# Queries and keys of the third pair of heads by seven products, with the token sums on GpSimd

## The chip, the cores and the metric

The kernel runs on one core of a Trainium2 chip. The metric is the device time of one execution in microseconds (us). In the profile the engines are PE (TensorE, the matmuls; PEld is its loading of weights), DVE (VectorE), ACT (ScalarE), POOL (GpSimd) and SP (SyncE, which issues most transfers).

## The reference

One layer of a hybrid backbone for two groups of tokens with the same weights: a prompt of 128 tokens and a sample of 512, D = 1024 channels, 16 heads of 64, all in float32. Cut to what matters:

```python
h = x * (1 + scale) + shift                        # modulation from the conditioning vector
z = h @ w_in                                       # 10 x 1024 columns: conv inputs, gates, q, k, v, merge gates
hy, g_h, qkv, g_a, m = split(z)
v_h, x1, x0 = split(short_conv(hy))                # 3 taps
y_h = (irfft(rfft(v_h * x1) * rfft(filter)) + (v_h * x1) * d_bias) * x0
q, k, v = split(qkv)
y_a = softmax(q k^T / 8 + bias, windows and context) v    # sample; the prompt attends to itself
p_h = (y_h * silu(g_h)) @ w_bh
p_a = (y_a * silu(g_a)) @ w_ba
m_h, m_a = split(sigmoid(m))
out = (m_h * p_h + m_a * p_a) @ w_out
y = layer_norm(ALPHA * x + gate * out)
```

The prompt's keys and values are outputs too.

## The kernel before

The 640 tokens are two halves of 320 columns (`HALF`, `CS`). The activations lie with channels on partitions, in 8 chunks of 128. A float32 operand is split into a high and a low part in the matmul's format (`hH`/`hL` for the tokens, `wh`/`wl` for weights), and each product is three passes: high x high, high x low, low x high. `split` makes the two parts, the high by a copy on ACT (L101), the low by a subtraction on DVE (L102).

There are two forms of projection onto a tile of 128 output channels. `proj` takes one weight tile: 8 chunks x 3 passes x 2 halves = 48 matmuls of 320 columns. `pair_tile` takes two weight tiles and both halves as a 2 x 2 block product and does it by seven products in place of eight: 7 x 4 chunks x 3 passes = 84 matmuls. It needs sums of the tokens, t1 to t4, made once and kept (`token_sums(r)`, where r = 0 or 1 picks chunks 0, 1 or 2, 3 of each half of the channels), sums of the weights (`wsum`, L1024, on DVE) with their splits, and sums of the results (L1058 to L1066, on DVE). The products come in the order `b11, t2, t3, t1, b21, t4, b22`; the split weights go round in a ring of buffers (`wh` has two, `wl` three), the raw weights have two buffers, which SP loads (`load_to`, L63).

The stages: a prologue makes h; four quarters of the convolution branch (`quarter_head`, `quarter_tail`, `long_conv`, `long_conv_back`; the products `yb` belong to the last step of the long convolution, and `conv_tile` reads a projection's result out of PSUM on ACT, L479 to L483, as zs); the hand-over; eight rounds of attention; the merge (projections `T_BH` and `T_BA`, gated by the merge gates, then the output projection); layer norm. Through the rounds `attend(j)`, two heads at a time, is woven into `mains(j)`, other projections that keep PE busy: scores (L819), probabilities (smallest value on DVE, L834; exponential on ACT, L839; reciprocal on DVE, L840; the multiply by it on GpSimd, L841, and L894 for the prompt), transposes (L859), values (L866). GpSimd does little else in this part.

The hand-over and round 0 are written so before:

```python
yield from chain(queries(0), keys(0), values(0), gate_a(0), queries(1))
yield from alongside(chain(keys(1), values(1)), token_sums(0), 2)          # end of hand_over
0: ((alongside(chain(gate_a(1), queries(2), keys(2)), token_sums(1), 2),), 3 * NK),   # mains(0)
1: ((mix(0), queries_keys(3)), 2 * N_PAIR),                                 # first pairs: round 1
```

`alongside(x, y, 2)` takes one step of y for two steps of x; `weave` spreads one chain over another by the numbers of steps given. The hand-over is woven with the end of the last long convolution.

What sets the order: each engine works through its own queue in order, and waits there for what the next instruction needs. In the rounds PE's queue is in the order written (`manual_schedule` for PE); the queues of the other engines there, and all of them in the convolution stages and the merge, are ordered by a scheduler when the kernel is built, except where `keep_in_program_order` pins an instruction. Weight tiles are named by number: `T_Q` = 32, `T_K` = 40, `T_V` = 48, `T_GA` = 56, `T_MH` = 64, `T_MA` = 72, `T_BH` = 80. The queries and keys of pair 2 are tiles 34 and 42, the first pair of the merge gates 64 and 65, gate_a(1) is tile 57.

Of the kernel before, what the change touches and what calls it, by code (L numbers as in the profile page):

```python
# [9 lines left out]
F32 = mybir.dt.float32  # L10
F32R = mybir.dt.float32r
AF = mybir.ActivationFunctionType
ALU = mybir.AluOpType
# [5 lines left out]
NK = 8  # L19
NT = 640  # L20
HALF = 320
# [24 lines left out]
def tile_hyena_natten_step(ctx: ExitStack, tc: tile.TileContext, a, o):  # L46
    nc = tc.nc
    P = 128

    def f(ap):  # L50
        return ap.bitcast(F32)
# [4 lines left out]
    def two(t):  # L56
        return t.rearrange("p (a b) -> p a b", a=2)
# [442 lines left out]
    def quarter_head(q):  # L500
        us = []
        out[f"u{q}"] = us
        for i in range(2):
            n = 2 * q + i
            u = hw.tile([P, NG + 1], F32, tag="u", bufs=4, name=f"u{n}")
            x1 = hwa.tile([P, NG + 1], F32, tag="cv", bufs=2, name=f"x1_{n}")
            yield from conv_tile(n, u)
            yield
            yield from conv_tile(8 + n, x1)
            nc.vector.tensor_tensor(u[:, :NG], u[:, :NG], x1[:, :NG], op=ALU.mult)  # L510
            us.append(u)
            yield
# [143 lines left out]
    def chain(*gens):  # L656
        for g in gens:
            yield from g
# [123 lines left out]
    def hand_over():  # L782
        yield from quarter_tail(3)
        hwa_stack.close()
        out["slots_l"] = left.enter_context(tc.tile_pool(name="slots_l", bufs=1))
        out["slots_q"] = left.enter_context(tc.tile_pool(name="slots_q", bufs=1))
        yield from chain(queries(0), keys(0), values(0), gate_a(0), queries(1))
        out["slots_r"] = left.enter_context(tc.tile_pool(name="slots_r", bufs=1))
        yield from alongside(chain(keys(1), values(1)), token_sums(0), 2)

    tail = ctx.enter_context(ExitStack())
    ac = ctx.enter_context(ExitStack())
# [172 lines left out]
    tok = {t: [[], []] for t in SUMS}  # L965

    def token_sums(r):
        def part(t, i, j):
            return f(t[:, 4 * i + 2 * r : 4 * i + 2 * r + 2, CS[j]])

        def step(dst, i, j, sign):
            for t in (hH, hL):
                nc.vector.tensor_tensor(dst, dst, part(t, i, j), op=ALU.add if sign > 0 else ALU.subtract)

        t1, t2 = (two(row(sp, "s", f"ts{r}{i}", bufs=2)[:]) for i in range(2))

        def keep(name, t):
# [4 lines left out]
            split(two(tok[name][0][r][:]), two(tok[name][1][r][:]), t)  # L982

        tc.keep_in_program_order(nc.vector.tensor_tensor(t1, part(hH, 0, 1), part(hL, 0, 1), op=ALU.add))
        yield
        nc.vector.tensor_tensor(t2, t1, part(hH, 0, 0), op=ALU.subtract)
        nc.vector.tensor_tensor(t2, t2, part(hL, 0, 0), op=ALU.subtract)
        yield
        keep("t1", t2)
        yield  # L990
        nc.vector.tensor_tensor(t1, part(hH, 1, 1), t1, op=ALU.subtract)
        nc.vector.tensor_tensor(t1, t1, part(hL, 1, 1), op=ALU.add)
        yield
        keep("t3", t1)
        yield
        step(t2, 1, 1, -1)
        yield
        keep("t2", t2)
        yield
        step(t2, 1, 0, 1)  # L1000
        yield
        keep("t4", t2)

# [6 lines left out]
    ORDER = ("b11", "t2", "t3", "t1", "b21", "t4", "b22")  # L1010
    RING = ("wh", "wl", "wl", "wh", "wl")

    def pair_tile(i0, i1, use):
        for i in (i0, i1):
            if i not in raws:
                wraw(i)
        ra, rb = raws.pop(i0), raws.pop(i1)
        a11, a12, a21, a22 = (r[:, 512 * h : 512 * h + 512] for r in (ra, rb) for h in range(2))
        src = {0: a11, 4: a12, 5: a22}
        wb = {}  # L1020

        def wsum(j, x, y, op, dst=None):
            src[j] = dst if dst is not None else row(sp, "s", f"s{j}_{i0}", bufs=2)[:, :512]
            nc.vector.tensor_tensor(src[j], x, y, op=op)  # L1024
# [7 lines left out]
        def halfrow(tag, bufs, name):  # L1032
            return sp.tile([P, 384], F32, tag=tag, bufs=bufs, name=f"{name}{i0}")[:, :HALF]

        wsum(2, a11, a21, ALU.subtract)
        wsum(1, src[2], a22, ALU.subtract)
        for j in range(3):
            prep(j)
        wsum(3, a21, a22, ALU.add)
        wsum(6, a12, src[1], ALU.add, src[1])  # L1040
        for j in range(3, 5):
            prep(j)
        ps = {}
        for j in range(7):
            if j < 4:
                ps["xyvz"[j]] = acc(f"sp{i0}_{j}")[:, :HALF]
            dst, x = ps["xyvzxvz"[j]], operand(ORDER[j])
            for k in range(4):
                wh, wl = (wb[j][:, i, P * k : P * k + P] for i in range(2))
                for i, (wk, xi) in enumerate(((wh, 0), (wh, 1), (wl, 0))):  # L1050
                    nc.tensor.matmul(  # L1051
                        dst, wk, x(xi, k), start=j < 4 and k == 0 and i == 0, stop=k == 3 and i == 2, skip_group_check=True,
                    )
                if k == 1:
                    yield
            if j == 0:
                u = halfrow("u", 1, "u")
                nc.scalar.activation(u, dst, AF.Copy)  # L1058
            elif j == 1:
                nc.vector.tensor_tensor(u, dst, u, op=ALU.add)  # L1060
            elif j == 4:
                use(0, 0, dst)
            else:
                if j != 3:
                    c = halfrow("c", 4, f"c{j}_")
                nc.vector.tensor_tensor(c, dst, c if j == 3 else u, op=ALU.add)  # L1066
                if j != 2:
                    use(*{3: (1, 1), 5: (1, 0), 6: (0, 1)}[j], c)
            prep(j + 5)
            yield  # L1070

    def queries_keys(j):
# [23 lines left out]
        yield from pair_tile(t0 + n0, t0 + n0 + 1, use)  # L1096

    N_PAIR = 14

    def alongside(main, side, every):  # L1100
# [76 lines left out]
    def gate_rows():  # L1177
        for k in range(NK):
            raw = slot(k % 2, "v", f"gate{k}")[:, :D]
            load_to(raw, a["wgate"][k])  # L1180
            yield
            for c in range(2):
                s_ = st[:, k, c : c + 1]
                if k == 0:
                    ins = nc.vector.tensor_scalar_mul(gbc[:, c], raw, s_)
                else:
                    ins = nc.vector.scalar_tensor_tensor(gbc[:, c], raw, s_, gbc[:, c], op0=ALU.mult, op1=ALU.add)
                if c == 0:
                    tc.keep_in_program_order(ins)

    wo = {}

# [24 lines left out]

    side = gate_rows()
    mhs = []
    for n in range(NK):  # L1220
        ps = now(proj(T_BH + n, yhH, yhL, dst=[[wo_row(t, 0, T_BH + n)] for t in ("woh", "wol")] if n == 2 else None))
        wraw(T_BH + n + 2)
        th = mixed(mh_d, n, "mh", NK)
        mhs.append(th)
        for p, cs in zip(ps, CS):
            gate(th[:, cs], p)
        raw = slot(1, ("q", "ql")[n % 2], f"yaraw{n}")
        load_to(raw[:], ya_d[n])
        split(yaH[n], yaL[n], raw[:])
        next(side, None)  # L1230
# [239 lines left out]
```

## Time and profile before

| | |
|---|---|
| median of 3 runs | 890.71 us (890.48 to 892.2) |
| profiled execution, its own time | 891.88 us |
| its span | 889.8 us |
| mean granted clock of TensorE in it | 0.995 |
| matmuls in the profile | 6536 with the transposes' and the attention's |
| bytes moved by DMA | 129.07 MB |

The busy share of each engine in 40 slices of the span, in tenths, shows the course: the convolution stages up to about slice 17, then the hand-over and the rounds, the merge from about slice 32.

```
PE   8999999999999999999999999999999999999996
DVE  4676693795678569698787667775777668676666
ACT  4395554645545433365666456555665632243200
POOL 0010110010101000025422322222222200000000
```

The page names an engine, a line of the kernel, an operation and "out<-in" tiles; `x12` is a count. In a list by time the first number is the start in us, the second the length of the row; in a list by groups, the numbers after the bar are the busy time in us and the mean length of one in ns. In brackets stands the idle time before and what ended it.

### The profile page before, as it was taken

How to read it: one execution, taken by the hardware profiler on the slowest of the kernel's cores; microseconds unless marked ns; L12 is line 12 of the kernel's file. 1: busy time of each engine (PE TensorE's matmuls, PEld its weight loads, DVE VectorE, ACT ScalarE, POOL GpSimd, SP SyncE). 2: the span in 40 equal slices, each digit the busy share in tenths (PEclk: the TensorE clock that was granted, in tenths of full speed). 3: DMA queues.
4: the chain of work that ended last, by engine and by line, in shares of the span. 5: the costliest groups of instructions: out<-in, count | busy, mean ns of one | idle time of the engine just before them, and what ended most of it. 6: DMA issues, size and time to landing. Idle time of an engine off the chain costs nothing.

```text
span 889.8 us, 16809 instructions
## 1 busy us (share of the span) xinstructions
PE 875.6 (98%) x6536; PEld 846.4 (95%) x6536; DVE 634.5 (71%) x1257; ACT 428.6 (48%) x912; POOL 121.6 (14%) x128
## 2 busy tenths in 40 slices
PE   8999999999999999999999999999999999999996
PEld 7899999999999999999999999999999999999885
DVE  4676693795678569698787667775777668676666
ACT  4395554645545433365666456555665632243200
POOL 0010110010101000025422322222222200000000
PEclk9999999999999999999999999999999999999998
DMA  8965665565656222263524243433252488445511
GB/s 329 395 163 122 142 141 119 143 135 120 160 113 142 72 85 76 72 193 101 157 83 141 88 139 104 148 104 113 84 169 92 140 298 283 154 153 201 209 61 58
DMA packets 53690, 129.07 MB, mean 145 GB/s; under 512 B 8267, under 2 KB 23115, under 8 KB 53612
## 3 DMA queue, kind: packets, MB, share of 16 engines
q1 hardware_dynamic: 43964, 107.72, 37.0%
q0 software_dynamic: 4032, 14.68, 10.1%
q10 hardware_dynamic: 5616, 5.61, 1.9%
q8 instruction: 51, 0.84, 0.4%
q14 instruction: 27, 0.22, 0.1%
HBM read 113.83 MB, written 14.16 MB: 144 GB/s over the span
## 4 chain that ended last, share of the span: by engine, by line
PE 91%; DMA 4%; DVE 3%; ACT 1%; issue 1%; SPq 0%; POOLq 0%; ACTq 0%; POOL 0%; DVEq 0%
PE mm L168 36%; PE sp L1051 20%; PE out L1285 6%; PE v L762 5%; PE mm L182 5%; PE pt L859 2%; DMA raw<-wall 2%; PE s L866 2%; PE s L819 2%; PE ve L774 1%; PE adaT L249 1%; DMA yhraw<-yh_d 1%; PE fl L397 1%; PE yb L158 1%; PE yb L156 1%; PE yb L157 1%
## 5 line engine op out<-in xcount | busy, mean ns | idle before, releaser
L1051 PE MATMUL sp<-t,wb 128*128 128x320 f32 x768 | 120.7, 310 | 0.1
L168 PE MATMUL mm<-hH,wh 128*128 128x320 f32 x480 | 115.0, 313 | 1.8 <-ACT zs L482 1.0
L1051 PEld LDWEIGHTS sp<-t,wb 128*128 128x128 f32 x768 | 113.8, 188 | 0.8 <-issue 0.8
L168 PE MATMUL mm<-hL,wh 128*128 128x320 f32 x480 | 114.4, 312 | 0.0
L168 PE MATMUL mm<-hH,wl 128*128 128x320 f32 x480 | 114.2, 312 | 0.0
L1051 PE MATMUL sp<-hH,wb 128*128 128x320 f32 x384 | 93.3, 313 | 1.1 <-DVE c L1066 1.1
L168 PEld LDWEIGHTS mm<-hH,wh 128*128 128x128 f32 x480 | 81.1, 189 | 3.9 <-ACT zs L482 1.2
L168 PEld LDWEIGHTS mm<-hL,wh 128*128 128x128 f32 x480 | 81.6, 189 | 1.1 <-DVE hL L326 0.5
L168 PEld LDWEIGHTS mm<-hH,wl 128*128 128x128 f32 x480 | 81.6, 189 | 0.8 <-DVE wl L102 0.4
L101 ACT ACTIVATE wh<-raw 128x1024 fp32r<-128x1024 f32 x33 | 34.8, 1058 | 73.6 <-PE mm L168 44.8
L1051 PEld LDWEIGHTS sp<-hH,wb 128*128 128x128 f32 x384 | 66.1, 188 | 3.2 <-issue 3.2
L148 POOL DMA_DIRECT2D wl<-wall x28 | 24.3, 869 | 262.7 <-ACT wl L147 225.0
L1051 PE MATMUL sp<-hL,wb 128*128 128x320 f32 x192 | 59.3, 309 | 0.0
L841 POOL TENSOR_SCALAR p<-p,sm 128x384 f32<-128x384 f32 x32 | 43.8, 1377 | 113.4 <-DVE sm L840 100.9
L102 DVE TENSOR_TENSOR wb<-s,wb 128x512 fp32r<-128x512 f32 x64 | 44.4, 699 | 20.6 <-ACT wb L101 20.5
L101 ACT ACTIVATE wb<-s 128x512 fp32r<-128x512 f32 x64 | 39.8, 628 | 34.6 <-DVE s L1024 30.6
L149 ACT ACTIVATE wh<-raw 128x1024 fp32r<-128x1024 f32 x28 | 29.7, 1061 | 52.8 <-PE mm L168 52.7
L102 DVE TENSOR_TENSOR wl<-raw,wh 128x1024 fp32r<-128x1024 f32 x33 | 40.2, 1220 | 13.6 <-ACT wh L101 13.2
L1285 PE MATMUL out<-woh,yhs 128*128 128x512 f32 (+1 forms) x176 | 45.5, 372 | 0.0
L841 POOL TENSOR_SCALAR edge<-edge,sm 128x320 f32<-128x320 f32 x32 | 41.7, 1315 | 2.6 <-DVE sm L840 2.6
L168 PE MATMUL mm<-yhs,wh 128*128 128x320 f32 x224 | 41.9, 309 | 0.0
L101 ACT ACTIVATE wb<-raw 128x512 fp32r<-128x512 f32 x48 | 30.0, 625 | 22.1 <-PE sp L1051 10.0
(357 smaller groups left out, 2155.0 us busy)
## 6 DMA issues: line engine op xcount, KB each, us to landing
raw<-wall SPq DMA_DIRECT2D x96, 512.0 KB, 3.7
wl<-wall POOLq DMA_DIRECT2D x28, 512.0 KB, 5.7
ada<-wada SPq DMA_DIRECT2D x16, 512.0 KB, 7.5
tm<-bias SPq DMA_DIRECT2D x16, 512.0 KB, 4.7
gate<-wgate SPq DMA_DIRECT2D x8, 512.0 KB, 4.4
wo<-wall SPq DMA_DIRECT2D x8, 512.0 KB, 4.3
xt<-xT SPq DMA_DIRECT2D x8, 320.0 KB, 7.5
dec<-decay SPq DMA_DIRECT2D x20, 128.0 KB, 3.3
```

What stands on the lines that cost most here:

```text
L101: hi = nc.scalar.activation(dst_h, src, AF.Copy)
L102: return hi, (eng or nc.vector).tensor_tensor(dst_l, src, f(dst_h), op=ALU.subtract)
L148: nc.gpsimd.dma_start(wl, a["wall"][i], accum_op=ALU.add)
L149: nc.scalar.activation(wh, raw[:], AF.Copy)
L168: nc.tensor.matmul(ps[hf][:, :HALF], wt[k], x[:, hf * HALF : (hf + 1) * HALF], start=(i == 0 and k == 0), stop=(i == lead[2] and k == NK - ...
L182: nc.tensor.matmul(p[:, :HALF], w[i // 2][k], (hH, hL)[i % 2][:, k, cs], start=n == 0, stop=n == len(steps) - 1, skip_group_check=True,)
L762: nc.tensor.matmul(ps[t // 2][:, t % 2 * 256 : t % 2 * 256 + 256], x[:, k, P * t : P * t + P], wk, start=first and t % 2 == 0, stop=last, ...
L819: nc.tensor.matmul(dst[h], x[rows(h), qs], y[rows(h), ks], start=i == 0, stop=i == 2, skip_group_check=True)
L841: nc.gpsimd.tensor_scalar_mul(pv, pv, sm[:, 2:3])
L859: nc.tensor.transpose(pt[:, i * P : i * P + P], x, ident)
L1051: nc.tensor.matmul(dst, wk, x(xi, k), start=j < 4 and k == 0 and i == 0, stop=k == 3 and i == 2, skip_group_check=True,)
L1285: ins = nc.tensor.matmul(dst, m[k][:, c0 : c0 + P], w[:, c : c + n], start=(first and k == 0), stop=(last and k == 5), skip_group_check=True,)
```

## The change

There are six edits.

1. Round 0 does `gate_a(1)` and then `queries_keys(2)`: the queries and keys of pair 2 as a pair by seven products, as those of pairs 3 to 7 are already.
2. The token sums of row pair 1 have to be there earlier. They are made in the hand-over, side by side with those of row pair 0 (`both`), on GpSimd in place of DVE: 18 operations of 128 x 320 (two per step of a row pair, since the temporaries are now rows of 384). The splits are in halves too: 8 copies on ACT, 8 subtractions on DVE. In the hand-over values(1) now stands ahead of keys(1).
3. `prepare` is the first part of `pair_tile`: loads of the two weight tiles, four weight sums and five splits. With the table `follow` the preparation for the following pair is issued after product 3 of the pair before, and its first weight sum is pinned in DVE's order. This holds inside the three runs of pairs that follow one another.
4. In `quarter_head` for q = 3 and i = 0 the two convolution tiles change places.
5. In the merge the first two T_BH projections are issued in a written order on PE: chunks 0 to 3 of both, then the rest.
6. `gate_rows` pins both of its operations in DVE's order, not the first alone.

```diff
@@ quarter_head
-            yield from conv_tile(n, u)
-            yield
-            yield from conv_tile(8 + n, x1)
+            tiles = ((n, u), (8 + n, x1))
+            if q == 3 and i == 0:
+                tiles = tiles[::-1]
+            yield from conv_tile(*tiles[0])
+            yield
+            yield from conv_tile(*tiles[1])
@@ hand_over
-        yield from alongside(chain(keys(1), values(1)), token_sums(0), 2)
+        yield from alongside(chain(values(1), keys(1)), both(token_sums(0), token_sums(1)), 2)
@@ token_sums(r)
+        eng = nc.gpsimd if r else nc.vector
+        if r:
+            temps = [
+                [sp.tile([P, 384], F32, tag="c", bufs=4, name=f"ts1{i}{k}")[:, :HALF] for k in range(2)] for i in range(2)
+            ]
+        else:
+            temps = [[two(row(sp, "s", f"ts0{i}", bufs=2)[:])] for i in range(2)]
...
+        def form(dst, x, terms):
+            for v, d in enumerate(dst):
+                y = x[v]
+                for t, i, j, sign in terms:
+                    eng.tensor_tensor(d, y, part(t, i, j, v), op=ALU.add if sign > 0 else ALU.subtract)
+                    y = d
...
+            for v, x in enumerate(src):
+                if r:
+                    cs = slice(HALF * v, HALF * v + HALF)
+                    split(th[:, cs], tl[:, cs], x)
+                else:
+                    split(two(th[:]), two(tl[:]), x)
...
+        form(t1, [part(hH, 0, 1, v) for v in range(len(t1))], ((hL, 0, 1, 1),))
+        form(t2, t1, ((hH, 0, 0, -1), (hL, 0, 0, -1)))
         keep("t1", t2)
+        for v, d in enumerate(t1):
+            eng.tensor_tensor(d, part(hH, 1, 1, v), d, op=ALU.subtract)
+        form(t1, t1, ((hL, 1, 1, 1),))
         keep("t3", t1)
+        form(t2, t2, ((hH, 1, 1, -1), (hL, 1, 1, -1)))
         keep("t2", t2)
+        form(t2, t2, ((hH, 1, 0, 1), (hL, 1, 0, 1)))
         keep("t4", t2)
@@ pair_tile
-    def pair_tile(i0, i1, use):
+    ready = {}
+
+    def prepare(i0, i1, pin):
         for i in (i0, i1):
             if i not in raws:
                 wraw(i)
...
-            nc.vector.tensor_tensor(src[j], x, y, op=op)
+            ins = nc.vector.tensor_tensor(src[j], x, y, op=op)
+            if pin and j == 2:
+                tc.keep_in_program_order(ins)
...
+        ready[i0] = wb, prep
+
+    def pair_tile(i0, i1, use):
...
+        if i0 not in ready:
+            prepare(i0, i1, False)
+        wb, prep = ready.pop(i0)
...
             prep(j + 5)
+            if j == 3 and (i0, i1) in follow:
+                prepare(*follow[i0, i1], True)
             yield
...
+    runs = (
+        (mix_(0), qk_(3), mix_(1), qk_(4), ga_(2)), (mix_(2), qk_(5), mix_(3), ga_(4), qk_(6)),
+        (mix_(4), qk_(7), mix_(5), ga_(6), mix_(6), mix_(7)),
+    )
+    follow = {x: y for run in runs for x, y in zip(run, run[1:])}
+
+    def both(x, y):
+        for _ in x:
+            next(y, None)
+            yield
+        yield from y
@@ mains(j)
-            0: ((alongside(chain(gate_a(1), queries(2), keys(2)), token_sums(1), 2),), 3 * NK),
+            0: ((gate_a(1), queries_keys(2)), NK + N_PAIR),
@@ gate_rows
-                if c == 0:
-                    tc.keep_in_program_order(ins)
+                tc.keep_in_program_order(ins)
@@ merge
+    firsts = [proj(T_BH + n, yhH, yhL) for n in range(2)]
+    with tc.manual_schedule(engines={mybir.EngineType.PE}):
+        for gen in firsts:
+            for _ in range(4):
+                next(gen)
+        firsts = [now(gen) for gen in firsts]
     for n in range(NK):
-        ps = now(proj(T_BH + n, yhH, yhL, dst=[[wo_row(t, 0, T_BH + n)] for t in ("woh", "wol")] if n == 2 else None))
+        if n < 2:
+            ps = firsts[n]
+        else:
+            ps = now(proj(T_BH + n, yhH, yhL, dst=[[wo_row(t, 0, T_BH + n)] for t in ("woh", "wol")] if n == 2 else None))
```

More of the change, by code (lines that the diff above doesn't have):

```diff
@@ L967, in token_sums, with part, keep @@
     def token_sums(r):
[L968 to L977, printed above, removed]
+        eng = nc.gpsimd if r else nc.vector
[5 more added lines that the diff above has]
+            temps = [[two(row(sp, "s", f"ts0{i}", bufs=2)[:])] for i in range(2)]
+        t1, t2 = temps
+        def part(t, i, j, v):
+            n = 4 * i + 2 * r
+            return f(t[:, n + v, CS[j]] if r else t[:, n : n + 2, CS[j]])
+        def form(dst, x, terms):
[4 more added lines that the diff above has]
+                    y = d
+        def keep(name, src):
             pools = [(yhp, "yh", NK + 1)] * 8 if r == 0 else [(tp, "tr", 4)] * 4 + [(sp, "tr", 3)] * 3 + [(at, "tr", 1)]
@@ L981, in keep @@
                 tok[name][i].append(row(pool, tag, f"{name}_{r}{i}", F32R, bufs))
-            split(two(tok[name][0][r][:]), two(tok[name][1][r][:]), t)
-        tc.keep_in_program_order(nc.vector.tensor_tensor(t1, part(hH, 0, 1), part(hL, 0, 1), op=ALU.add))
+            th, tl = (tok[name][i][r] for i in range(2))
+            for v, x in enumerate(src):
[5 more added lines that the diff above has]
+        form(t1, [part(hH, 0, 1, v) for v in range(len(t1))], ((hL, 0, 1, 1),))
         yield
-        nc.vector.tensor_tensor(t2, t1, part(hH, 0, 0), op=ALU.subtract)
-        nc.vector.tensor_tensor(t2, t2, part(hL, 0, 0), op=ALU.subtract)
+        form(t2, t1, ((hH, 0, 0, -1), (hL, 0, 0, -1)))
         yield
@@ L990, in token_sums @@
         yield
-        nc.vector.tensor_tensor(t1, part(hH, 1, 1), t1, op=ALU.subtract)
-        nc.vector.tensor_tensor(t1, t1, part(hL, 1, 1), op=ALU.add)
+        for v, d in enumerate(t1):
+            eng.tensor_tensor(d, part(hH, 1, 1, v), d, op=ALU.subtract)
+        form(t1, t1, ((hL, 1, 1, 1),))
         yield
@@ L995, in token_sums @@
         yield
-        step(t2, 1, 1, -1)
+        form(t2, t2, ((hH, 1, 1, -1), (hL, 1, 1, -1)))
         yield
@@ L999, in token_sums @@
         yield
-        step(t2, 1, 0, 1)
+        form(t2, t2, ((hH, 1, 0, 1), (hL, 1, 0, 1)))
         yield
@@ L1030, in prep @@
             split(wb[j][:, 0], wb[j][:, 1], src[j])
-        def halfrow(tag, bufs, name):
-            return sp.tile([P, 384], F32, tag=tag, bufs=bufs, name=f"{name}{i0}")[:, :HALF]
         wsum(2, a11, a21, ALU.subtract)
@@ L1042, in pair_tile, with halfrow @@
             prep(j)
+        ready[i0] = wb, prep
+    def pair_tile(i0, i1, use):
+        def halfrow(tag, bufs, name):
+            return sp.tile([P, 384], F32, tag=tag, bufs=bufs, name=f"{name}{i0}")[:, :HALF]
+        if i0 not in ready:
+            prepare(i0, i1, False)
+        wb, prep = ready.pop(i0)
         ps = {}
@@ L1098, in tile_hyena_natten_step, with qk_, ga_, mix_ @@
     N_PAIR = 14
+    def qk_(j):
+        return T_Q + j, T_K + j
+    def ga_(j):
+        return T_GA + j, T_GA + j + 1
+    def mix_(m):
+        t = (T_MH if m < 4 else T_MA) + 2 * (m % 4)
+        return t, t + 1
+    runs = (
[8 more added lines that the diff above has]
+        yield from y
     def alongside(main, side, every):
```

## The prediction

> **What bounds the kernel now.** I read the share of busy time first, then the chain that ended last, then the list of what TensorE (PE) waited for.
>
> ```profile
> PE 875.6 (98%) x6536; PEld 846.4 (95%) x6536; DVE 634.5 (71%) x1257; ACT 428.6 (48%) x912; POOL 121.6 (14%) x128
> PE 91%; DMA 4%; DVE 3%; ACT 1%; issue 1%; SPq 0%; POOLq 0%; ACTq 0%; POOL 0%; DVEq 0%
> ```
>
> ```profile
> engine line waited for: us in total, times, longest us
> PE adaT L266 <- POOL spare L281: 1.5, 1, 1.5
> PE sp L1051 <- DVE c L1066: 1.1, 1, 1.1
> PE mm L168 <- ACT zs L482: 1.0, 1, 1.0
> PE pt L859 <- DVE sm L834: 0.6, 1, 0.6
> ```
>
> PE is busy for 98% of the span and carries 91% of the chain. So only two things can move the time: fewer matmuls, or PE waiting less or more. Three waits behind the prologue are worth having: 1.1 us at a pair's product, 1.0 at a convolution tile and 0.6 at the attention's transposes.
>
> Shares over the whole span hide the stage that the change touches, so I looked at it by windows (columns: length, then busy time of PE, PEld, DVE, ACT, POOL).
>
> ```profile
> 372.00:397.00 25.00, 25.00 (x204) 24.37 (x204) 24.19 (x49) 11.78 (x30) 1.59 (x6) 1.00 0.58 189
> 397.00:404.80 7.80, 7.25 (x55) 6.83 (x55) 7.80 (x23) 4.20 (x11) 7.57 (x4) 1.00 0.28 77
> 404.80:415.00 10.20, 10.20 (x71) 10.10 (x72) 7.73 (x16) 5.72 (x16) 5.77 (x5) 1.00 0.31 105
> ```
>
> This is the end of the hand-over and round 0, up to the first product of pair 64. DVE works 24.19 of 25.00 us and then 7.80 of 7.80, and GpSimd (POOL) 7.57 of 7.80. PE is still full, but with two engines behind it that have nothing left. All the new work of the change falls here.
>
> **Twelve matmuls fewer.** Queries and keys of pair 2 cost 2 x 48 matmuls of 320 columns now, and 7 products x 4 blocks x 3 passes = 84 in the new form.
>
> ```profile
> 491.70 1.92 PE L1051 MATMUL sp<-t,wb 128*128 128x320 f32 x12
> 493.45 0.31 PE L1051 MATMUL sp<-hH,wb 128*128 128x320 f32 x1
> ```
>
> Twelve run from 491.70 to 493.45, 1.75 us, or 0.146 each. Gain: 12 x 0.146 = 1.75 us. That is 0.2% of the time, which is also about what a measurement of this kernel can tell from no change (1.78 us).
>
> **Stalls that the small edits take away.** The swapped order of the convolution tiles at q 3, i 0 puts other matmuls between ACT's reading of the held PSUM tile and PE's next use of it. I take all of the 1.0 us of zs L482; the cover is some fifty matmuls, and if it were gone, the 1.0 would stay.
>
> ```profile
> 574.44 0.69 DVE L1024 TENSOR_TENSOR s<-raw,raw 128x512 f32<-128x512 f32 x1 [3.86 <-DMA raw<-wall]
> 576.41 0.38 PE L1051 MATMUL sp<-hH,wb 128*128 128x320 f32 x1 [1.08 <-DVE c L1066]
> ```
>
> At 574.44 DVE stands 3.86 us before a weight sum whose tile has not landed, the combination L1066 that PE needs is queued behind it, and PE loses 1.08 us. With `prepare` the following pair's loads, sums and splits are issued after product 3 of the pair before, in a written place. The load then is earlier by about three products (some 5 us at 1.75 each), more than the 3.86, so I take the 1.1 us whole. SP's queue gets the same loads, sooner. The other pairs keep their slack: what they get earlier is one split and two sums on a DVE that isn't full there. The written order of the first two T_BH projections and the second pin in `gate_rows` touch a wait too small for the list: nothing counted, with some 0.4 us as the upper bound (an estimate, half a small wait of the list) and zero as the lower. The 0.6 us at L859 lies inside the stage that is built anew: its present form goes, and what comes in its place is the next term. Gains so far: 1.75 + 1.0 + 1.1 + 0.6 = 4.45 us.
>
> **What the hand-over has to do instead.** `token_sums(1)` leaves round 0 on DVE and becomes 18 GpSimd operations of 128x320 in the hand-over, 8 ACT copies and 8 DVE splits of half a row pair. Into DVE's queue also come the sums and splits of the weights of pair 34/42, which PE now wants at once.
>
> ```profile
> 372.12 0.28 PE L158 MATMUL yb<-ph,dftL 128*128 128x256 f32 x1
> 388.90 0.46 PE L182 MATMUL mm<-hH,wh 128*128 128x320 f32 x2
> 399.01 0.46 PE L182 MATMUL mm<-hH,wh 128*128 128x320 f32 x2
> 372.79 0.82 DVE L984 TENSOR_TENSOR ts<-hH,hL 128x640 f32<-128x640 f32 x1
> 375.24 0.82 DVE L991 TENSOR_TENSOR ts<-hH,ts 128x640 f32<-128x640 f32 x1
> 375.98 0.60 DVE L630 SCALAR_TENSOR_TENSOR u<-u,hyd,yp 128x128 f32<-128x128 f32 x2
> 394.88 0.55 DVE L834 CUSTOM_DVE_ANT_0 p<-s,tm 128x384 f32<-128x384 f32 x1
> L102 DVE TENSOR_TENSOR wb<-s,wb 128x512 fp32r<-128x512 f32 x64 | 44.4, 699 | 20.6 <-ACT wb L101 20.5
> ```
>
> The token sums follow the last `yb` of the long convolution. In the changed order of issue 113 matmuls stand between it and gate_a(1), some 14.5 us, so with gate_a(1) at 388.90 it falls at 374.4, where before it fell at 372.12: values(1), ahead of keys(1) now, fill the place. DVE starts its sums 2.3 us later. PE's frame is kept: gate_a(1) with its scores ends at 399.01, the first product of queries and keys takes 12 x 0.146, and the second wants its weights and the sums t2 at 400.8. Before that DVE has 64 operations to do, which by their rows (0.82 for a sum or split of 640, about half of that for 320, 0.70 for a weight operation of 512, 0.55 for a probability step) come to 31 us, or about 27 when overlaps of 0.07 us between neighbours are taken off (the operation of 375.24 has its successor at 375.98). 374.4 + 27 = 401.4 to 402.4: DVE alone is 0.6 to 1.6 us late, without any disturbance. I take 1.5.
>
> GpSimd's part has no such operation in the trace. The nearest are these:
>
> ```profile
> L841 POOL TENSOR_SCALAR edge<-edge,sm 128x320 f32<-128x320 f32 x32 | 41.7, 1315 | 2.6 <-DVE sm L840 2.6
> 442.19 2.14 POOL L841 TENSOR_SCALAR edge<-edge,sm 128x320 f32<-128x320 f32 x2 [0.64 <-DVE sm L840]
> 397.23 4.52 POOL L841 TENSOR_SCALAR edge<-edge,sm 128x320 f32<-128x320 f32 x2 [1.35 <-DVE sm L840]
> 401.73 6.10 POOL L841 TENSOR_SCALAR p<-p,sm 128x384 f32<-128x384 f32 x4
> 407.81 2.76 POOL L841 TENSOR_SCALAR edge<-edge,sm 128x320 f32<-128x320 f32 x2
> L1314 POOL TENSOR_TENSOR r<-r,bc 128x64 f32<-128x64 f32 x1 | 0.3, 319 | 175.9 <-ACT r L1313 175.9
> L1315 POOL TENSOR_TENSOR r<-r,bc 128x64 f32<-128x64 f32 x1 | 0.6, 612 | 0.1
> 403.42 0.82 PE L859 MATMUL pt<-pack,edge 128*128 128x128 f32 x6
> 404.79 0.93 PE L859 MATMUL pt<-pack,p 128*128 128x128 f32 x6 [0.56 <-DVE sm L834]
> 404.98 1.01 DVE L1024 TENSOR_TENSOR s<-raw,raw 128x512 f32<-128x512 f32 x1
> ```
>
> A multiply of this size takes 1.07 us alone (442.19), 1.3 on average, and (4.52 + 2.76) / 4 = 1.82 beside a full DVE; DVE's own 512-column sum is longer there too, 1.01 against about 0.70. The only two tensor-tensor rows, of 64 columns, scatter by a factor of two. So an operation costs between 1.07 and 1.82, and I take 1.5, nearer to the crowded rows since DVE is as full here. 18 x 1.5 = 27 us from 374.8: GpSimd is through at 402, where undisturbed (18 x 1.07 = 19.3) it would be at 394 or, with its two waits for DVE's splits of t1 and t2, at 396. Behind these eighteen are queued the attention's multiplies, which began at 397.23 before and feed the transposes at 403.42 and 404.79; DVE's and ACT's halves of `t*_1` wait for GpSimd in their own order, and behind ACT's halves stand the copies that free PSUM for keys(1). So GpSimd is some 5 us late for the multiplies, and what DVE loses to it, some 0.15 us for each of 18 operations (2.6 us, worked out from 0.3 us for every DVE operation that meets one, about half of them), comes partly on top. Of 1.5 + 5 + 2.6 I take 7 us as PE's loss, since the waits lie beside one another in part. Bounds: at 1.3 each the loss is 18 x 0.23 = 4.1 us, at 1.82 it is 18 x 0.75 = 13.5 less some 1 us of slack, 12.5.
>
> [...]
>
> Sum: 7.0 - 4.45 = +2.5 us. The profiled execution took 891.88 us, 2.1 more than its span, and would become 894.4; it lies 1.17 above the median of the three runs, 890.71, and on that scale the forecast is **893.2 us**.
>
> **The rivals.**
>
> *A cheap hand-over.* If the eighteen operations run at 1.07 us or less and hardly disturb DVE, GpSimd is done at 396 at the latest, ahead of its multiplies, and only DVE's own lateness of 1.5 with some 0.5 of disturbance is left: 2.0 - 4.45 = -2.5, 888.2 us. For it speaks that outside the crowded stage the pairs of 320 take 2.14 (442.19); against it that this stage is crowded. It decides below about 1.2 us for an operation. [...]
>
> *DVE and GpSimd take turns.* If a two-input operation on one engine wholly holds up the other's, GpSimd's operations run at 1.82 or above and DVE's as much later; PE waits at keys(1), at the scores of blocks 2 and 3 and at the second product, 12.5 us in all: +8, 898.7 us. This is the slow side by one mechanism, with its place in 374 to 402 and from about 1.8 us for an operation. For it speak the 4.52 us for two at 397.23; against it that DVE's operations there lengthen by 0.3 and not by a whole multiply. [...]
>
> *The small edits don't do what they say.* The loads of `prepare` come no earlier because their buffers are still held, and the tile swap moves the PSUM wait elsewhere: then only 1.75 + 0.6 stands against 7, 895.4 us. The 3.86 us on a DMA speaks for a load that is simply late in the queue, so I hold this unlikely.
>
> **How the numbers follow.** The forecast (loss 5 to 9.5, its own range 891 to 896 us) gets 0.48, the cheap hand-over 0.36 (886.5 to 889.7), taking turns 0.12 (896 to 902), and edits without effect 0.04. The range leaves out the lower part of the second and the upper part of the third: 887.2 to 899.0. Faster by over 0.2% (below 888.9): 0.32 of the cheap case and 0.02 from the forecast's edge, 0.34. Within 0.2% (up to 892.5): 0.04, 0.13 of the forecast and 0.01 of the last case, 0.18. Slower: 0.33 + 0.12 + 0.03 = 0.48.
>
> **What would show it.** Matmuls: 12 fewer in the program, and L1051's counterparts 84 more. The waits on zs L482 and on c at the product near 576 are gone from PE's list. In the windows from 372 to 405 POOL becomes busy for 25 us or more, PE loses some 7, in front of keys(1), the scores of blocks 2 and 3, and the transposes or the second product; GpSimd's 128x320 tensor-tensor reads 1.3 to 1.7 us. A mean below 1.2 with PE losing under 3 us there makes the cheap case right, one of 1.8 or more the third. I am wrong in another way if PE loses time in later rounds, where nothing here is counted.

## The result, and the profile after

The changed kernel takes 895.05 us (median of 6 runs, 894.78 to 896.3), the kernel before in the same comparison 891.09 us. The ratio is 1.0043 (95% interval 1.0029 to 1.0057): about 4 us slower. The profiled execution took 896.3 us with a span of 894.4, against 891.88 and 889.8.

The shares on the page of the changed kernel (its lines are later by 3 in the attention and by 30 at the pairs' products, now L1081):

```profile
PE 876.2 (98%) x6524; PEld 846.4 (95%) x6524; DVE 643.6 (72%) x1266; ACT 432.2 (48%) x921; POOL 145.3 (16%) x146
```

The list of PE's waits, without those of the prologue (us in total, times, longest):

```profile
PE mm L182 <- ACT v L772: 4.6, 1, 4.6
PE s L822 <- DVE sm L837: 1.3, 1, 1.3
PE pt L862 <- POOL p L844: 0.6, 1, 0.6
PE pt L862 <- DVE sm L837: 0.3, 1, 0.3
PE pt L862 <- DVE sm L843: 0.2, 1, 0.2
```

The twelve matmuls are gone (6536 to 6524), the waits on `zs L482` and on `c` at a pair's product too. In their place stands one wait of 4.6 us: PE at the second half of keys(1), for ACT's copy of the values v1 out of PSUM. In it and behind it the windows show something that before has only in its prologue (0.50 from 12 to 14 us) and at its very end (0.50 from 886 on): a low granted clock. The columns are length, then busy time of PE, PEld, DVE, ACT, POOL, then the granted clock:

```profile
385.00:386.00 1.00, 0.00 (x0) 0.00 (x0) 1.00 (x5) 0.00 (x0) 0.05 (x1) 0.93 0.00 0
386.00:387.00 1.00, 0.00 (x0) 0.00 (x0) 1.00 (x4) 0.14 (x1) 0.06 (x1) 0.50 0.07 26
388.20:390.20 2.00, 1.98 (x7) 1.98 (x8) 2.00 (x4) 2.00 (x8) 0.37 (x1) 0.50 1.05 257
390.20:392.20 2.00, 2.00 (x9) 2.00 (x9) 2.00 (x8) 1.06 (x4) 2.00 (x1) 0.50 0.97 378
392.70:394.00 1.30, 1.30 (x11) 1.30 (x10) 1.28 (x2) 0.63 (x1) 1.22 (x2) 1.00 1.04 418
```

The granted clock falls to 0.50 while PE still waits, and for about 4.5 us after the wait PE runs at half its clock. The timelines of DVE, GpSimd and ACT in the stage (start and length in us):

```profile
373.25 1.50 DVE L988 TENSOR_TENSOR ts<-hH,hL 128x640 f32<-128x640 f32 x1
377.48 1.50 DVE L1011 TENSOR_TENSOR ts<-hH,ts 128x640 f32<-128x640 f32 x1
379.42 2.25 DVE L642 SCALAR_TENSOR_TENSOR u<-u,hyd,y 128x512 f32<-128x512 f32 x2
382.84 1.50 DVE L102 TENSOR_TENSOR t<-ts,t 128x640 fp32r<-128x640 f32 x1
384.26 1.15 DVE L468 TENSOR_TENSOR yh<-yh,u 128x128 f32<-128x128 f32 x2
385.33 1.42 DVE L472 TENSOR_TENSOR yh<-yh,u 128x64 f32<-128x64 f32 x4
386.67 0.81 DVE L988 TENSOR_TENSOR ts<-ts,hH 128x640 f32<-128x640 f32 x1
372.67 2.80 POOL L988 TENSOR_TENSOR ts<-hH,hL 128x320 f32<-128x320 f32 x2 [86.03 <-PE yb L158]
375.43 2.87 POOL L988 TENSOR_TENSOR ts<-ts,hH 128x320 f32<-128x320 f32 x2
380.51 0.89 POOL L988 TENSOR_TENSOR ts<-ts,hL 128x320 f32<-128x320 f32 x1
382.19 2.86 POOL L988 TENSOR_TENSOR ts<-ts,hL 128x320 f32<-128x320 f32 x2
386.86 0.83 ACT L101 ACTIVATE t<-ts 128x320 fp32r<-128x320 f32 x2 [2.23 <-DVE yh L472]
387.60 1.06 ACT L772 ACTIVATE v<-v 128x512 f32<-128x512 f32 x2
```

While GpSimd works (372.67 to 385.0), each DVE operation of 640 columns that reads two tensors, neither of them out of PSUM, takes 1.4 to 1.5 us in place of 0.82, and each of GpSimd's beside one of them some 1.4; at 386.67, with GpSimd idle, DVE is back at 0.81. Both advance by one operation per 1.4 us. Beside `L642`, which reads one of its two tensors out of PSUM, neither loses: its two operations take 2.25 us (2.22 before), and GpSimd's there 0.88 or 0.89 each. The step that matters is `L472`, the end of the convolution on DVE. The tiles of the hand-over lie where the convolution's tiles lay, so ACT's first copy into them waits for it. Before:

```profile
380.50 1.41 DVE L472 TENSOR_TENSOR yh<-yh,u 128x64 f32<-128x64 f32 x4
382.03 0.56 ACT L726 ACTIVATE k<-mm 128x64 fp32r<-128x64 f32 x3 [1.82 <-DVE yh L472]
```

There the copies waited too (for k1), but PE had values(1) to do meanwhile. L472 started at 380.50 then and at 385.33 now, 4.83 us later: 0.46 because DVE begins later, 3.7 from six operations of 640 columns that sum to 8.62 us in place of 4.88, and 0.7 at L468.

Landmarks in PE's timeline, in us from the span's start, close the account:

| first matmul of | before | after | difference |
|---|---|---|---|
| the products of tile 64 (round 1) | 415.24 | 421.03 | +5.79 |
| tile 38 (with 46, round 5) | 578.24 | 582.39 | +4.15 |
| the last pair (tile 78) | 693.60 | 698.65 | +5.05 |
| the output projection | 825.86 | 830.52 | +4.65 |

Up to tile 64, the swapped convolution tile is worth 1.8 and the matmuls 1.75, so the hand-over and round 0 lost 5.79 + 3.55 = 9.3 us: 4.8 at keys(1), 2.05 by the half clock (4.5 us of it), 1.7 at the scores of block 2, and some 0.8 in smaller pieces; the gap at the transposes stands at 0.58 (0.56 before). The prepared weights then give 1.6 back by tile 38, 0.9 is lost in the last round, most of it at transposes, and 0.4 is won in the merge.

### The profile page after: what moved, and what is told of

The parts are those of the page before. It is cut to its first block, busy times and chain, and to the rows that moved or that the text cites. A ratio compares the mean times of both kernels' runs of the same rounds, so it can differ in the third digit from the quotient of the medians.

```text
span 894.4 us, 16798 instructions
## 1 busy us (share of the span) xinstructions
PE 876.2 (98%) x6524; PEld 846.4 (95%) x6524; DVE 643.6 (72%) x1266; ACT 432.2 (48%) x921; POOL 145.3 (16%) x146
## 4 chain that ended last, share of the span: by engine, by line
PE 91%; DVE 5%; DMA 1%; ACT 1%; POOL 1%; issue 1%; POOLq 0%; ACTq 0%; DVEq 0%
PE mm L168 37%; PE sp L1081 21%; PE out L1347 6%; PE v L765 5%; PE mm L182 4%; PE s L869 2%; PE pt L862 2%; PE s L822 2%; PE ve L777 1%; PE adaT L249 1%; DVE ts L988 1%; DMA raw<-wall 1%; PE adaT L266 1%; DVE wb L102 1%; PE fl L397 1%
## 5 line engine op out<-in xcount | busy, mean ns | idle before, releaser
L1081 PE MATMUL sp<-t,wb 128*128 128x320 f32 x816 | 128.7, 311 | 0.0
L1081 PEld LDWEIGHTS sp<-t,wb 128*128 128x128 f32 x816 | 121.0, 188 | 0.9 <-issue 0.5
L168 PE MATMUL mm<-hH,wl 128*128 128x320 f32 x480 | 112.2, 310 | 0.4 <-DVE wl L102 0.4
L1081 PE MATMUL sp<-hH,wb 128*128 128x320 f32 x408 | 98.8, 313 | 0.0
L1081 PEld LDWEIGHTS sp<-hH,wb 128*128 128x128 f32 x408 | 70.2, 188 | 1.9 <-issue 1.9
L1081 PE MATMUL sp<-hL,wb 128*128 128x320 f32 x204 | 63.0, 309 | 0.0
L101 ACT ACTIVATE wh<-raw 128x1024 fp32r<-128x1024 f32 x31 | 32.7, 1057 | 55.3 <-PE mm L168 19.5
L102 DVE TENSOR_TENSOR wb<-s,wb 128x512 fp32r<-128x512 f32 x68 | 46.7, 701 | 16.6 <-ACT wb L101 16.6
L149 ACT ACTIVATE wh<-raw 128x1024 fp32r<-128x1024 f32 x28 | 29.7, 1061 | 50.6 <-PE mm L168 50.6
L102 DVE TENSOR_TENSOR wb<-raw,wb 128x512 fp32r<-128x512 f32 x51 | 36.6, 718 | 13.3 <-ACT wb L101 12.4
L102 DVE TENSOR_TENSOR wl<-raw,wh 128x1024 fp32r<-128x1024 f32 x31 | 37.8, 1221 | 11.6 <-ACT wh L101 11.4
```

The lines of the kernel that those rows point to most:

```text
L101: hi = nc.scalar.activation(dst_h, src, AF.Copy)
L102: return hi, (eng or nc.vector).tensor_tensor(dst_l, src, f(dst_h), op=ALU.subtract)
L149: nc.scalar.activation(wh, raw[:], AF.Copy)
L168: nc.tensor.matmul(ps[hf][:, :HALF], wt[k], x[:, hf * HALF : (hf + 1) * HALF], start=(i == 0 and k == 0), stop=(i == lead[2] and k == NK - ...
L1081: nc.tensor.matmul(dst, wk, x(xi, k), start=j < 4 and k == 0 and i == 0, stop=k == 3 and i == 2, skip_group_check=True,)
```

## The experiments

Ratios are to the kernel before in the same comparison, with 95% intervals.

**1. The small edits alone.**

```diff
-            0: ((gate_a(1), queries_keys(2)), NK + N_PAIR),
+            0: ((alongside(chain(gate_a(1), queries(2), keys(2)), token_sums(1), 2),), 3 * NK),
-        yield from alongside(chain(values(1), keys(1)), both(token_sums(0), token_sums(1)), 2)
+        yield from alongside(chain(keys(1), values(1)), token_sums(0), 2)
```

(with `token_sums` as before)

> The kernel with edits 3 to 6 alone (prepared weights, swapped convolution tiles, written merge order, both pins); pair 2 and the token sums as before. The landmarks of the two traces put the small edits at -1.65 us (convolution tile), -1.32 (prepared weights, at tile 60) and -0.4 (merge), and one new loss at +0.9 (transposes near 684). If these terms are independent of the pair, it is 2.5 us faster than before, ratio 0.9972 (0.996 to 0.9985). If they were only shifts that the later stall brought about, ratio 0.999 to 1.001.

Measured: 889.68 us, ratio 0.9974 (0.9961 to 0.9988). The size is as expected, the parts are not. Its list of waits:

```profile
PE ve L777 <- DVE kl L737: 1.6, 1, 1.6
```

This wait is new. PE comes some 1.8 us earlier to the end of values(1) and waits there for DVE's split of k1, so the gain of the convolution tile was given back at once: tile 64 starts only 0.1 us sooner than before (both reckoned from the first filter product, to leave the prologue out). What is left comes from the prepared weights (1.6 us up to tile 72, with 0.3 lost behind it) and the merge (0.4). DVE was the bound of the hand-over already before, hidden by a PE that was just as late.

**2. Weights prepared in one run only.**

```diff
-    runs = (
-        (mix_(0), qk_(3), mix_(1), qk_(4), ga_(2)), (mix_(2), qk_(5), mix_(3), ga_(4), qk_(6)),
-        (mix_(4), qk_(7), mix_(5), ga_(6), mix_(6), mix_(7)),
-    )
+    runs = ((mix_(2), qk_(5), mix_(3), ga_(4), qk_(6)),)
```

(on the first experiment)

> As the one before, but the following pair is prepared ahead only in the second of the three runs of pairs (tiles 68 to 46), where the 1.1 us wait was. If the +0.9 near 684 comes from the third run's preparation, which puts weight work into DVE's queue ahead of the attention's, it is gone and the kernel is 3.4 us faster than before, ratio 0.9962. If that loss has another source (the shift of the merge's loads), it stays and the ratio is 0.9972 as in the one before.

Measured: 889.73 us, ratio 0.9972 (0.9959 to 0.9985). In the trace the stretch from tile 72 to the last pair is as long as before (80.93 us), where the first experiment had 81.25 and the changed kernel 81.83. So preparing the third run does cost 0.3 us, and more in kernels that come to it otherwise shifted: the stretch is 80.93 or 80.94 us in all three that leave it out (experiments 2, 5 and 9) and 81.25 to 82.69 in all that have it. The times cannot tell the first two experiments apart, and the ratio of 0.9962 expected for this outcome is not reached, since 0.3 us went and not 0.9. The 1.6 us wait is the same.

**3. GpSimd reads one tensor.**

```diff
-                    eng.tensor_tensor(d, y, part(t, i, j, v), op=ALU.add if sign > 0 else ALU.subtract)
+                    if r:
+                        eng.tensor_scalar_mul(d, y, out["hyd"][:, 0:1])
+                    else:
+                        eng.tensor_tensor(d, y, part(t, i, j, v), op=ALU.add if sign > 0 else ALU.subtract)
```

(and the same for the first step of t3)

> The whole change, but each of the 18 GpSimd operations reads one tensor (times a column) in place of two; the token sums of row pair 1 are thereby left out. Theory A (DVE and GpSimd take turns at reading two tensors): DVE's sums of 640 go back from 1.4 to 1.5 us to 0.82 to 0.95, the convolution's last step on DVE (L472) ends about 4 us sooner, the 4.6 us wait of PE at keys(1) falls under 1.5 and the clock stays at 1.00 there; total about 889 to 891, ratio 0.998 to 1.000. Theory B (any GpSimd operation holds DVE up as much): the stage stays as it is, ratio 1.004. Theory C (not the contention but the chain of GpSimd itself is too long): DVE's operations get short, but the wait at the scores and transposes stays, ratio about 1.002.

Measured: 895.37 us, ratio 1.0027 (1.0008 to 1.0046). The first half of theory A holds, the time does not follow it. Timelines of DVE, GpSimd and ACT:

```profile
373.35 0.82 DVE L991 TENSOR_TENSOR ts<-hH,hL 128x640 f32<-128x640 f32 x1
375.19 1.05 DVE L991 TENSOR_TENSOR ts<-ts,hL 128x640 f32<-128x640 f32 x1
381.44 1.41 DVE L472 TENSOR_TENSOR yh<-yh,u 128x64 f32<-128x64 f32 x4
379.94 7.61 POOL L1015 TENSOR_SCALAR ts<-ts,pack 128x320 f32<-128x320 f32 x1
388.64 0.47 ACT L101 ACTIVATE t<-ts 128x320 fp32r<-128x320 f32 x1 [5.20 <-POOL ts L989]
389.01 1.06 ACT L772 ACTIVATE v<-v 128x512 f32<-128x512 f32 x2
```

DVE now has the upper hand: 0.80 to 1.05 for its sums, and L472 at 381.44. But one GpSimd operation of 1.08 us took 7.61, through a stretch in which DVE read two tensors almost without a break; it ended 0.95 us after the last of these (386.60). ACT's copy of t1 waited 5.2 us for GpSimd, and the copies of v1 stood behind it in ACT's queue, so PE waited 5.9 us at the same place, and the half clock came too. The wait had changed its cause: ACT's order, no longer L472.

**4. The sums on DVE.**

```diff
-        eng = nc.gpsimd if r else nc.vector
+        eng = nc.vector
```

> The whole change, but the token sums of row pair 1 are made by DVE, in the same place and the same halves. Theory A: without turns DVE's sums of row pair 0 cost 0.82 again, but its queue has 18 operations of about 0.45 us more (8 us), about what the turns cost it; PE's wait at keys(1) is 3 to 5 us with a later one at the second product of tile 34, in all 893 to 897, ratio 1.002 to 1.006. Theory D (it is GpSimd alone that is at fault, DVE had room): ratio below 1.000.

Measured: 897.07 us, ratio 1.0051 (1.0033 to 1.007), as theory A said. DVE's sums of row pair 0 are back at 0.82 to 0.85, and its 18 of half size take 0.48 to 0.52 (means of the trace's groups). From PE's list of waits:

```profile
PE mm L182 <- ACT v L772: 3.2, 1, 3.2
PE s L822 <- DVE sm L837: 2.2, 2, 1.8
PE sp L1081 <- DVE wb L102: 2.0, 1, 2.0
```

and the window behind the first of these waits:

```profile
386.50:392.00 5.50, 5.48 (x44) 5.29 (x45) 5.50 (x15) 4.01 (x13) 0.00 (x0) 1.00 1.01 331
```

The same work in DVE's own queue costs at least as much as the turns did. GpSimd as such is not the fault: the hand-over has no room for these sums on either engine. The clock stays at 1.00 after the wait of 3.2 us; it falls to 0.50 later, from 409.07 to 412.48, behind waits of 2.7 us in all at the products of tile 34.

**5. Values first, no new sums.**

```diff
-        yield from alongside(chain(keys(1), values(1)), token_sums(0), 2)
+        yield from alongside(chain(values(1), keys(1)), token_sums(0), 2)
```

(on the second experiment)

> As the second experiment (edits 3 to 6, the preparation in the second run alone), but with values(1) ahead of keys(1) in the hand-over, and no sums on GpSimd. There PE waited 1.8 us at the end of values(1) for DVE's split of keys(1), which took back the 1.65 us of the swapped convolution tile: the hand-over was then bound by DVE. Theory Q (DVE's queue, up to the convolution's last step L472 and what follows it, has no slack): with values in front, keys(1) is no longer wanted so early, the 1.8 us wait goes and some 0.5 to 1 comes back at the transposes: ratio 0.995 to 0.9965. Rival (values first is itself what made PE wait at keys(1) for the copies of v1): a wait of 2 us or more at keys(1), ratio 0.9985 to 1.000.

Measured: 888.73 us, ratio 0.9959 (0.9944 to 0.9974), the fastest kernel here with nothing left out. Theory Q holds: the 1.6 us wait is gone, and 0.9 us stands at the transposes for ACT's copies, where it was 0.3. The order of values and keys, edited along with the sums in the change, is itself a gain. The intervals of this and the second experiment overlap; the traces show it, where tile 64 starts 0.8 us sooner than in the second and the output projection 0.45 (from the first filter product). With DVE undisturbed the copies of v1 come 5 us sooner than in the changed kernel, and PE does not wait for them (ACT's timeline):

```profile
382.42 1.09 ACT L772 ACTIVATE v<-v 128x512 f32<-128x512 f32 x2 [0.85 <-DVE yh L472]
```

**6. The sums on GpSimd, the pair as before.**

```diff
-            0: ((gate_a(1), queries_keys(2)), NK + N_PAIR),
+            0: ((gate_a(1), queries(2), keys(2)), 3 * NK),
```

(on the changed kernel)

> The whole change, but queries(2) and keys(2) by 48 matmuls each as before; the token sums of row pair 1 stay on GpSimd in the hand-over. Theory A (the loss is the GpSimd sums beside DVE): the 4.6 us wait at keys(1) and the low clock behind it stay, the wait at the scores of block 2 falls from 1.7 to 0 to 1, and 12 matmuls come back (1.76): ratio 1.003 to 1.006. Rival (the loss is the weight work of pair 34/42 in DVE's queue): the waits go, ratio 0.997 to 1.000.

Measured: 894.96 us, ratio 1.0026 (1.0016 to 1.0037), at the low edge. The 4.6 us wait at keys(1) stays to the tenth, and so does the half clock (386.64 to 393.47), so the sums beside DVE make them. The waits at the scores and at the first transposes go wholly, so with 12 matmuls more this kernel reaches tile 64 some 1.1 us sooner than the changed one. The pair's own 1.75 us was thus more than eaten. That its weight work in DVE's queue did it, where the splits of the new sums stand too, is argued from the waits and not shown by itself; experiment 9, without those sums, keeps the gain there.

**7. The new sums three steps later.**

```diff
-        yield from alongside(chain(values(1), keys(1)), both(token_sums(0), token_sums(1)), 2)
+        yield from alongside(chain(values(1), keys(1)), both(token_sums(0), chain(iter(range(3)), token_sums(1))), 2)
```

> The whole change, with token_sums(1) written three steps later, which puts ACT's copies of v1 ahead of the copies t1_1 in its queue; GpSimd's operations are the same and start as early. Theory L (the copies of v1 need a place in memory that DVE's last step of the convolution, L472, sets free, and that step is late by the lengthened sums): PE's wait at keys(1) stays at 4 to 5 us, ratio 1.003 to 1.005. Theory O (the copies of v1 are held only by their place behind t1_1, which waits for GpSimd): the wait falls under 1.5 and the low clock goes, ratio 0.996 to 0.999.

Measured: 897.51 us, ratio 1.0056 (1.004 to 1.0073). ACT's timeline:

```profile
386.57 1.09 ACT L772 ACTIVATE v<-v 128x512 f32<-128x512 f32 x2 [2.21 <-DVE yh L472]
```

The windows behind the restart of PE at 387.22:

```profile
387.30:388.50 1.20, 1.20 (x8) 1.20 (x9) 1.20 (x2) 1.20 (x4) 0.00 (x0) 1.00 1.02 329
388.65:392.30 3.65, 3.65 (x17) 3.65 (x16) 3.65 (x11) 2.90 (x9) 2.00 (x2) 0.53 0.95 309
```

The copies of v1 stand first on ACT now and still wait for L472; PE waits 3.9 us. Theory L is right for the changed kernel, O is not. The half clock comes here too, 1.4 us after PE's restart (388.66 to 392.08), and once more from 409.14 to 412.56, behind the waits at tile 34 told below. The later sums miss the second product of tile 34, where PE waits 2.8 us more; the ratio is a little above the expected band.

**8. One tensor, three steps later.**

The two edits of experiments 3 and 7 together.

> The third experiment (one tensor read by each GpSimd operation; the sums of row pair 1 are left out) with token_sums(1) written three steps later. There DVE's operations kept their 0.82 us and L472 was done at 382.8, but one GpSimd operation took 7.6 us beside DVE, and the copies of v1 stood behind it on ACT. With them in front, L and O both say that the wait at keys(1) goes (under 1.5 us) and the clock stays at 1.00; what is left is the lateness of GpSimd's chain at the second product of tile 34, 2 to 4 us. Ratio 0.996 to 1.000. If the wait at keys(1) stays, neither is right.

Measured: 893.61 us, ratio 1.0017 (1.0008 to 1.0027); the wait at keys(1) is 0.4 us, and no low clock follows there. Two lines of its waits:

```profile
PE sp L1087 <- ACT wb L101: 1.3, 1, 1.3
PE mm L182 <- ACT v L772: 0.4, 1, 0.4
```

So the two causes at keys(1) are both found: L472 where GpSimd reads two tensors, ACT's order where it reads one and starves. The total is worse than I expected, since PE waits 3.0 us in all at the products of tile 34, runs at half its clock amid these waits (401.92 to 405.33), against the 1.00 that I expected, and waits 1.1 us at transposes in the last round.

**9. The pair without its sums.**

```diff
-            0: ((alongside(chain(gate_a(1), queries(2), keys(2)), token_sums(1), 2),), 3 * NK),
+            0: ((gate_a(1), queries_keys(2)), NK + N_PAIR),
-            return lambda i, k: tok[name][i][k // 2][:, HALF * (k % 2) : HALF * (k % 2) + HALF]
+            return lambda i, k: tok[name][i][0][:, HALF * (k % 2) : HALF * (k % 2) + HALF]
```

(on the fifth experiment)

> The fifth experiment (values first, small edits) with the queries and keys of pair 2 by seven products, and no token sums of row pair 1 at all: the products of all pairs read those of row pair 0 in their place, so that 18 operations and 4 splits are left out. This is the bound for the idea: the pair with its sums for nothing. If the sums are the whole loss, it is faster than the fifth experiment by the 12 matmuls (1.76 us) and by the 0.5 to 1.5 us of waits at transposes and pairs that a freer DVE saves: ratio to before 0.993 to 0.9945. If the pair's weights (sums and splits on DVE in round 0) are themselves part of the loss, PE waits at the second product of tile 34 and the ratio is 0.995 or above.

Measured: 887.34 us, ratio 0.9947 (0.9928 to 0.9966), between the two bands that were expected; PE does not wait at the second product of tile 34. Tile 64 starts 3.4 us sooner than in the fifth experiment, but 1.4 us of it go again at one product near 480 us, where PE waits 1.8 us for DVE's split of q in place of 0.4. By the traces, the bound of the idea is about 1.3 us under the fifth experiment, with all its sums for nothing; the intervals of the two ratios overlap.

**10. Ten of the eighteen operations.**

```diff
-                for t, i, j, sign in terms:
+                for t, i, j, sign in terms[:1] if r else terms:
-        form(t1, t1, ((hL, 1, 1, 1),))
+        if not r:
+            form(t1, t1, ((hL, 1, 1, 1),))
```

> The whole change with 10 of the 18 GpSimd operations (the second term of each sum, and a step of t3, are left out). Theory A (every GpSimd operation takes its turn with a DVE operation and costs DVE about 0.6 us): ahead of L472 DVE loses 4.6 us now; with 6 instead of 11 operations there it loses about 2.5, PE's wait at keys(1) is 2 to 3 us, too short for the low clock (a wait of 3.4 us was, one of 4.0 was not), so that 2 us more come back: 4 us in all, ratio 0.999 to 1.001. Theory B (the start or the last GpSimd operation decides, not their number): ratio 1.003 to 1.0045.

Measured: 892.59 us, ratio 1.0007 (0.9995 to 1.002). The timelines of DVE and GpSimd:

```profile
377.34 1.50 DVE L1011 TENSOR_TENSOR ts<-hH,ts 128x640 f32<-128x640 f32 x1
378.11 2.30 POOL L1011 TENSOR_TENSOR ts<-hH,ts 128x320 f32<-128x320 f32 x2
381.41 0.83 DVE L988 TENSOR_TENSOR ts<-ts,hL 128x640 f32<-128x640 f32 x1
```

PE's wait, and the window behind it:

```profile
PE mm L182 <- ACT v L772: 2.7, 1, 2.7
```

```profile
386.20:391.90 5.70, 5.70 (x21) 5.70 (x22) 5.65 (x13) 4.03 (x12) 4.09 (x2) 0.50 1.01 347
```

Theory A by dose: DVE takes 1.5 us as long as GpSimd works and 0.83 from the operation after; the wait is 2.7 us. The clock I had wrong: reckoned from experiment 4 (3.2 us in its list of waits, 1.00 behind it) and experiment 7 (3.9 us, then 0.50), it should have stayed; it fell in this shorter wait as well, and stood at 0.50 for some 6 us behind it. The time came out right since the wait at the scores was gone too.

## Why the prediction was right, and where not

The forecast was 893.2 us, +2.5 on the scale of the first runs; measured was +4.0, inside the range and on the forecast side. By its steps:

- **Twelve matmuls, 1.75 us.** The count is right. As a gain it never arrived: experiment 6 shows round 0 faster without the pair.
- **Stalls removed, 1.0 + 1.1 + 0.6.** The first two waits went, with 1.8 and 1.6 us by the landmarks. The gap at the transposes kept its length, so the 0.6 was no gain. But experiment 1 shows that of the first, nothing is left without the values moved ahead: the prediction read PE's wait as PE's loss, where the stage behind it was bound by DVE to within 0.1 us. The windows of before had said so, 24.19 of 25.00.
- **"The other pairs keep their slack."** Wrong by 0.9 us, in the last round. Experiment 2 ties at least 0.3 of it to the third run's preparation, and no kernel without that preparation loses here; what makes it more in the changed kernel is open.
- **The merge:** 0.4 us, the upper bound given.
- **Where the sums start.** I put the last `yb` at 374.4, by counting matmuls in the changed order. It stands at 372.24 as before; the values were taken out of the stretch behind it too. The sums began some 2 us earlier than I said (GpSimd's at 372.67, not 374.8).
- **GpSimd's operation, 1.5 us.** The 18 sum to 24.2 us in four groups of the trace, 1.34 each, in the foretold 1.3 to 1.7; beside `L642` it takes 0.88.
- **What DVE loses to one operation, 0.15 us.** This is the term that was mis-sized: it is 0.55 to 0.68, four times as much, since the rows that I took it from (multiplies that read one tensor) are not of the kind. Experiment 3 shows that kind beside the same sums: 0 to 0.23 us a sum. So the engines do take turns here, the mechanism of my third case, one operation each per 1.4 us, though at 1.34 us an operation and not at the 1.8 that I gave as its sign. The turns are even only up to 385 us: at 389.83 one GpSimd operation took 3.00 us. In experiment 3, where GpSimd read one tensor, it was GpSimd that was kept out: 7.6 us for an operation of 1.08. The turns are not whole: a sum of DVE advances by 0.74 us alone (375.24 to 375.98 before) and GpSimd's operation takes 0.88 beside `L642`, and these 1.62 us of work in 1.4 us of time leave some 0.2 us in which the two overlap, an estimate from these rows.
- **Loss of the stage, 7 us; measured 9.3.** I placed it in the multiplies and transposes behind GpSimd. It came at keys(1) through L472, which no step of mine names, and through the clock. GpSimd was through at 401.6, as forecast (402), but gate_a(1) itself began 4.95 us late by then (393.85), so its lateness was hardly felt: the gap at the transposes is 0.58 us, and none stands at the second product.

The chance of 0.48 for the forecast and 0.12 for the turns belong together: the mechanism was the latter's, and the size, 9.3 us, lay between their 7 and 12.5. That the time came out on the forecast's side with the loss in another place and from another cause is in part luck.

## What to carry to other kernels

DVE, busy for 24.2 of 25 us beside a full PE, was a bound too: the 1.8 us won ahead of it were given back at its next result (a wait of 1.6 us in experiment 1), and more work had no place there, neither in its own queue (experiment 4, ratio 1.0051) nor on GpSimd beside it (1.0043). Before moving elementwise work to GpSimd, look in the trace for a DVE operation with two inputs beside a GpSimd operation of the same kind (here 1.4 to 1.5 us in place of 0.82), and not merely beside any (0.80 to 1.05 in experiment 3). And when two tiles change places, look for whose memory they take: here the order of values and keys alone, with the small edits, is a ratio of 0.9959, while the pair with its sums was a loss.

## What the runs showed of the hardware

A short idle of PE cost its clock too, in five of the seven kernels below. The waits at the end of the hand-over and what the windows show after them:

| PE waits | granted clock after it |
|---|---|
| 1.6 us (experiment 1) | 1.00 |
| 3.2 us (experiment 4) | 1.00 |
| 2.7 us (experiment 10) | 0.50 for some 6 us |
| 3.9 us (experiment 7) | 1.00 for 1.4 us, then 0.50 to 392.1 |
| 4.6 us (changed kernel) | 0.50 for 4.5 us |
| 4.6 us (experiment 6) | 0.50 for 4.9 us |
| 5.9 us (experiment 3) | 0.50 for 3.3 us |

So length alone does not decide it: 3.2 us left the clock at 1.00 and 2.7 us did not. Nor does the fall always come within the wait. In the changed kernel PE stood from 383.6 to 388.2 and the clock read 0.50 from 385.86 to 392.69; in experiment 7 PE was at work again from 387.22, and the clock read 0.50 from 388.66 to 392.08. In the prologue of before it fell at 11.32 us, with PE busy for 1.10 of the 1.30 us from 10.00 to 11.30. What sets the start and the length of these stretches is not shown here.
